# Attention of two heads at a time: scores alternate between the array's row halves, values between its column halves

## The chip, the cores and the metric

One core of one Trainium2 chip runs the whole program. The metric is the device time of one execution in microseconds (us). Three runs of the kernel before took 1670.49, 1671.25 and 1674.58 us, a median of 1671.25 us.

## The reference, cut to what matters

The program is a stack of transformer blocks on 256 tokens of width 1024, all in float32, batch 1. Two layers of the first kind are feed-forward, mixer, feed-forward, each with a residual; two layers of the second kind are one mixer each. The first mixer has three branches, the second has two attentions and a convolution. Heads are 64 wide everywhere, apart from MLA, whose queries and keys are 96 wide:

```
first mixer, a layer:   MLA 6 heads (q, k 96 wide, v 64), MOBA 6 heads,
                        dilated: 4 heads x 3 patterns, joined over the patterns by their log-sum-exp
second mixer, a layer:  FOX 4 heads (bias from cumulated forget gates),
                        NSA 8 heads x 2 sets of keys (selected, window), plus compressed keys
every one of these:     s = q @ k.T * scale + bias;  p = softmax(s, causal);  o = p @ v
```

With 256 tokens MOBA's and NSA's selections hold all blocks, so each attention is a causal one with its own bias. That makes 24 softmax tables of 256x256 per layer in the first mixer (6 + 6 + 12) and 20 in the second (4 + 16), 88 in all.

## The kernel before, in words

**Stages.** The order is feed-forward, first mixer, feed-forward, twice, then the second mixer twice and a last norm (`STAGES`). Every big product is made exactly enough by splitting both operands in two float32r parts and running three matmuls (`mm3`, L229, and `mm3w`, L235; their matmuls are L231 to L233 and L239 to L241). Weights come through one stream (`Stream.emit`, L92): a DMA on SyncE's queue into a `raw` tile of 128x1024, a copy by ScalarE to the high part (`wh`, L110), a subtraction by VectorE to the low part (`wl`, L111). Seven such chunks are kept under way.

**Order.** The Tile framework orders instructions itself: it gives each engine a fixed list, in program order where nothing is waited for by its own timing model, with later instructions put in where an earlier one is not ready. On the chip every engine then runs its list in order. Lower priority is given to the weights' splits (`LOW`). So the projections that stand between attention heads fill the gaps of the heads' chains.

**One head.** `scores` (L534) takes a bank of PSUM from the tag `xt`, of which there are three, and writes the causal half of the table into it: 128 queries against 128 keys (L537) and the other 128 queries against 256 keys (L538). Both are plain float32 matmuls, which the trace records as two passes each. For a head of 64 the operands lie on partitions 0 to 63 or 64 to 127, by the head's parity, so the matmul uses half of the array's rows. `biased` (L543) adds the bias on VectorE and finds the minimum (L546), which frees the bank; `exps` (L552) is ScalarE's Exp (L554); `weighted` (L557) scales the rows on VectorE (L559). `values` (L561) transposes three 128x128 blocks on TensorE into another `xt` bank (L244), copies them to SBUF (ScalarE at L570, for some dilated tables VectorE at L572) into one of two `pt` buffers, and multiplies them with v (L573 and L574), which is 64 columns wide: the output goes to partitions 0 to 63 or 64 to 127 of the one `ot` bank that a pair of heads shares (`pair_out`, L609).

**Lag of one.** `attend` (L576) emits the scores and softmax of a head and then the values of the head before it:

```python
    def attend(self, job):
        first, second = job
        first()
        self.settle()
        self.waiting = second
```

A dilated head does three tables (`dil_job`, L777), with three `p` tiles of six, an NSA head two (`nsa_job`, L1157). After a pair's second head the output bank is split in two parts (L247, L248) or gated (L1154).

**Order around the change.** In the first mixer (L865 to L887) MLA's pairs stand between projections, then MOBA's, then the four gates of branch 0, `dil_pair(0)`, the four gates of branch 1, `dil_pair(1)`, the rest of the values, the four gates of branch 2. A gate (`gated`, L833) is 48 matmuls of gate and some of branch. In the second mixer (L1353 to L1374) FOX and NSA pairs stand between projections, convolution taps on VectorE (`conv`, L1265) and the output product (`outs`).

Of the kernel before, what the change touches and what calls it, by code (L numbers as in the profile page):

```python
# [17 lines left out]
EPS = 1e-6  # L18
# [58 lines left out]
class Stream:  # L77
    """Weights in the order of their use: loaded, and split exactly in two float32r parts."""
# [21 lines left out]
            # a feed-forward's own weights also take turns in the buffers that its pool adds  # L100
# [21 lines left out]
class Next:  # L122
    """what follows a phase, for one block of 128 tokens"""
# [18 lines left out]
class Kernel:  # L142
# [27 lines left out]
    # ------------------------------------------------------------ tiles  # L170
# [32 lines left out]
    def p384(self):  # L203
        return self.lent.tile([128, 384], F32, name="p", bufs=6)
# [23 lines left out]
    # ------------------------------------------------------------ helpers  # L228
# [47 lines left out]
    def setup(self):  # L276
        """what the mixers need"""
# [10 lines left out]
        # rows to columns: the taps, conv_b, ln_g, ln_b of both layers, position embeddings, latent gains  # L288
# [62 lines left out]
    def finish_phase(self, step, n, accs, factor, nxt):  # L351
        """the last n steps of a sum, token block by token block, with the next norm between them"""
# [20 lines left out]
    # ------------------------------------------------------------ feed-forward  # L373
# [21 lines left out]
    def ffn(self, src, pre, nxt, phase, mid):  # L395
# [5 lines left out]
        def finish(j, ga, ua, natural):  # L401
            """silu(gate) * up of 256 columns, transposed and split"""
# [80 lines left out]
    def xs_spec(self, w, c0, n):  # L483
        """the same with the activations stationary"""
# [5 lines left out]
    def ws_proj(self, src, done, i, each=None):  # L490
        """256 columns, transposed: done(i, psum [128, 2, 256])"""
# [12 lines left out]
    def xs_proj(self, src, n, done, pre=None, each=None):  # L504
        """n columns, tokens on partitions: done(t, psum [128, n])"""
# [37 lines left out]
    def biased(self, p, st, table, scale, low):  # L543
        """p = (scores + table) * scale, which is minus the logits; low [128, 2]: their minima"""
# [16 lines left out]
    def values(self, o, p, v, first, last, evac):  # L561
        """o [64, 256] += v.T @ p.T for p [128, 384]"""
        nc = self.nc
        pt = self.xt()
        self.transpose(pt[:, 0:128], p[:, 0:128])
        self.transpose(pt[:, 128:256], p[:, 128:256])
        self.transpose(pt[:, 256:384], p[:, 256:384])
        ps = self.lent.tile([128, 384], F32, name="pt", bufs=2)
        if evac == "a":
            nc.scalar.copy(ps, pt[:, :384])  # L570
        else:
            nc.vector.tensor_copy(ps, pt[:, :384])  # L572
        nc.tensor.matmul(o, lhsT=v[0], rhs=ps[:, 0:256], start=first, stop=False)  # L573
        nc.tensor.matmul(o[:, 128:256], lhsT=v[1], rhs=ps[:, 256:384], start=False, stop=last)  # L574
# [13 lines left out]
    def head(self, q, k, v, o, table, scale, end=None, evac="a"):  # L588
        """o(): psum [64, 256] for the values"""
        p, s = [], []  # L590

        def first():
            st = self.scores(q, k)
            p.append(self.p384())
            s.append(self.small())
            t = table() if callable(table) else table
            self.biased(p[0], st, t, scale, s[0][:, 0:2])
            self.exps(p[0], s[0][:, 0:2], s[0][:, 2:4])
            self.nc.vector.reciprocal(s[0][:, 4:6], s[0][:, 2:4])
            self.weighted(p[0], s[0][:, 4:6])  # L600

        def second():
            self.values(o(), p[0], v, True, True, evac)
            if end:
                end()
# [3 lines left out]
    def pair_out(self):  # L609
        """one psum tile for two heads, made when the first asks for it"""  # L610
# [9 lines left out]
    def rope_pairs(self, a, b, cos, sin, shape):  # L620
        """(a, b) = (a cos - b sin, a sin + b cos) in place"""
# [33 lines left out]
    def mixer1(self, l, src, pre, nxt, mid):  # L655
# [3 lines left out]
        # latent projections, their norms, the shared rotated key  # L659
# [29 lines left out]
        # MOBA queries and keys, transposed, two heads to a block  # L689
# [16 lines left out]
        # MLA heads  # L706
# [48 lines left out]
        def mla_pair(p):  # L755
            o = self.pair_out()
            for m in range(2):
                h = 2 * p + m
                v = [vv[:, t, 64 * h:64 * h + 64] for t in range(2)]
                self.attend(self.head(qT[0:96, h], kT[0:96, h], v, lambda m=m: o(m), self.table(4), 1.0,  # L760
                                      (lambda: finish(0, p, o())) if m else None))

        bv = self.g(9408, 2, 384)

        def moba_pair(p):
            o = self.pair_out()
            for m in range(2):
                h = 2 * p + m
                r = slice(64 * m, 64 * m + 64)
                v = [bv[:, t, 64 * h:64 * h + 64] for t in range(2)]  # L770
                self.attend(self.head(bq[r, p], bk[r, p], v, lambda m=m: o(m), self.table(0), SLOPES[12 + h],
                                      (lambda: finish(1, p, o())) if m else None))
# [4 lines left out]
        def dil_job(p, m, o):  # L777
            j = 2 * p + m
            r = slice(64 * m, 64 * m + 64)
            pp = []  # L780

            def first():
                pp.extend(self.p384() for _ in range(3))
                s = self.small(24)
                low = s[:, 0:6].rearrange("p (g b) -> p g b", b=2)
                den = s[:, 6:12].rearrange("p (g b) -> p g b", b=2)
                for g in range(3):
                    sc = self.scores(dq[r, 2 * g + p], dk[r, 2 * g + p])
                    self.biased(pp[g], sc, self.table(1 + g), SLOPES[4 * g + j], low[:, g])
                lo, dn = s[:, 12:14], s[:, 14:16]  # L790
                nc.vector.tensor_reduce(lo, s[:, 0:6].rearrange("p (g b) -> p b g", b=2), op=OP.min, axis=AX.X)
                for g in range(3):
                    self.exps(pp[g], lo, den[:, g])
                nc.vector.tensor_reduce(dn, s[:, 6:12].rearrange("p (g b) -> p b g", b=2), op=OP.add, axis=AX.X)
                nc.vector.reciprocal(dn, dn)
                for g in range(3):
                    self.weighted(pp[g], dn)

            def second():
                for g in range(3):  # L800
# [672 lines left out]
```

## Time and profile before

| what | value |
|---|---|
| runs, us | 1670.49, 1671.25, 1674.58 |
| span of the profiled execution | 1671.4 us |
| TensorE matmul busy | 1625.8 us, 97% |
| TensorE weight load busy | 1472.4 us, 88% |
| VectorE busy | 1027.7 us, 61% |
| ScalarE busy | 813.5 us, 49% |
| mean DMA rate | 162 GB/s |

The profiled execution's span stands 0.15 us above the median of the runs, so span and time are taken as one. In the trace a matmul has a start and a modelled end; the ends of neighbours overlap, so the cost of one is read from its start to the start of the next, not from its duration. A form such as 64*128 64x256 is the used rows and columns of the array, then partitions and elements of the output's operand.

### The profile page before, as it was taken

What the parts mean: (1) busy time and instruction counts of PE and PEld (TensorE: products, weight loads), DVE (VectorE), ACT (ScalarE), POOL (GpSimd) and SP (SyncE); (2) the same over time, 40 slices, a digit from 0 to 9 for tenths busy, and PEclk for the clock granted to TensorE, in tenths of its full rate; (3) what the DMA queues carried; (4) which work ended last, traced back from release to release, by engine and by line L of the source; (5) the groups of instructions that cost most, each with busy time, mean ns of one, the idle gap of its engine ahead of it and who ended that gap; (6) DMA issues with size and microseconds to landing.
All of it is one profiled execution on the core that took longest, in us unless ns stands there. A gap on an engine that the chain in (4) does not pass through costs nothing.

```text
span 1671.4 us, 28176 instructions
## 1 busy us (share of the span) xinstructions
PE 1625.8 (97%) x11210; PEld 1472.4 (88%) x11210; DVE 1027.7 (61%) x1896; ACT 813.5 (49%) x1365; POOL 70.4 (4%) x76
## 2 busy tenths in 40 slices
PE   6999999999999999999999999999999989999998
PEld 6899999799989999999999799889999788778875
DVE  6655465566675545645456546676544779777885
ACT  5544355554464444444435545555443554555353
POOL 0000000001000000000010000000000011000300
PEclk9999999999999999999999999999999999999999
DMA  8866455344577664766636444477664463246411
GB/s 274 261 187 193 117 168 147 109 140 129 183 214 221 189 186 143 225 186 190 178 97 182 121 136 140 129 222 242 185 190 139 143 201 121 58 122 206 140 43 39
DMA packets 212508, 271.41 MB, mean 162 GB/s; under 512 B 10382, under 2 KB 188440, under 8 KB 212376
## 3 DMA queue, kind: packets, MB, share of 16 engines
q1 hardware_dynamic: 211944, 268.56, 54.0%
q8 instruction: 88, 1.44, 0.4%
q10 hardware_dynamic: 432, 1.05, 0.2%
q14 instruction: 44, 0.36, 0.1%
HBM read 268.52 MB, written 1.05 MB: 161 GB/s over the span
## 4 chain that ended last, share of the span: by engine, by line
PE 83%; DVE 7%; DMA 4%; ACT 2%; issue 2%; POOL 1%; SPq 0%; DVEq 0%; POOLq 0%; ACTq 0%
PE acc L239 16%; PE acc L241 15%; PE acc L240 15%; PE xt L231 4%; PE xt L233 4%; PE xt L232 4%; PE xt L244 3%; PE ot L573 3%; PE acc L231 3%; PE acc L232 3%; PE acc L233 3%; DVE wl L111 2%; PE xt L538 2%; PE xt L537 2%; DMA raw<-in_ffn_w_gate_dram 1%
## 5 line engine op out<-in xcount | busy, mean ns | idle before, releaser
L111 DVE TENSOR_TENSOR wl<-raw,wh 128x1024 fp32r<-128x1024 f32 (+6 forms) x510 | 607.2, 1194 | 449.8 <-ACT wh L110 438.7
L110 ACT CAST wh<-raw 128x1024 fp32r<-128x1024 f32 (+5 forms) x520 | 525.5, 1013 | 589.6 <-PE acc L240 346.7
L239 PE MATMUL acc<-hl,wh 128*128 128x256 f32 x2080 | 594.6, 286 | 0.0
L240 PE MATMUL acc<-hh,wh 128*128 128x256 f32 x2080 | 591.6, 284 | 0.0
L241 PE MATMUL acc<-hh,wl 128*128 128x256 f32 x2080 | 591.2, 284 | 0.0
L239 PEld LDWEIGHTS acc<-hl,wh 128*128 128x128 f32 x2080 | 398.3, 191 | 5.5 <-issue 4.0
L241 PEld LDWEIGHTS acc<-hh,wl 128*128 128x128 f32 x2080 | 398.3, 191 | 4.0 <-issue 4.0
L240 PEld LDWEIGHTS acc<-hh,wh 128*128 128x128 f32 x2080 | 398.3, 191 | 3.2 <-issue 1.7
L231 PE MATMUL acc<-wh,hl 128*128 128x256 f32 (+5 forms) x576 | 189.9, 330 | 2.9 <-DVE hl L248 1.1
L232 PE MATMUL acc<-wh,hh 128*128 128x256 f32 (+5 forms) x576 | 186.2, 324 | 0.0
L233 PE MATMUL acc<-wl,hh 128*128 128x256 f32 (+5 forms) x576 | 185.9, 323 | 0.0
L231 PEld LDWEIGHTS acc<-wh,hl 128*128 128x128 f32 x576 | 109.9, 191 | 13.7 <-issue 3.7
L233 PEld LDWEIGHTS acc<-wl,hh 128*128 128x128 f32 x576 | 109.8, 191 | 6.8 <-issue 1.0
L232 PEld LDWEIGHTS acc<-wh,hh 128*128 128x128 f32 x576 | 110.0, 191 | 6.2 <-issue 1.0
L231 PE MATMUL xt<-wh,R 128*128 128x512 f32 x264 | 103.8, 393 | 1.3 <-DVE R L248 1.3
L232 PE MATMUL xt<-wh,R 128*128 128x512 f32 x264 | 103.5, 392 | 0.0
L233 PE MATMUL xt<-wl,R 128*128 128x512 f32 x264 | 103.3, 391 | 0.0
L554 ACT ACTIVATE p<-p,small 128x128 f32<-128x128 f32 (+1 forms) x176 | 78.6, 448 | 26.8 <-DVE small L546 17.2
L546 DVE CUSTOM_DVE_ANT_0 p<-xt,base 128x128 f32<-128x128 f32 (+1 forms) x160 | 50.9, 352 | 19.0 <-PE xt L538 18.3
L570 ACT COPY pt<-xt 128x384 f32<-128x384 f32 x80 | 37.5, 474 | 49.2 <-PE xt L244 48.0
L231 PEld LDWEIGHTS xt<-wh,R 128*128 128x128 f32 x264 | 49.6, 188 | 11.6 <-DVE R L248 2.3
L233 PEld LDWEIGHTS xt<-wl,R 128*128 128x128 f32 x264 | 49.6, 188 | 10.6
(253 smaller groups left out, 1806.9 us busy)
## 6 DMA issues: line engine op xcount, KB each, us to landing
raw<-in_w_in_dram SPq DMA_DIRECT2D x144, 512.0 KB
raw<-in_ffn_w_gate_dram SPq DMA_DIRECT2D x88, 512.0 KB
raw<-in_ffn_w_up_dram SPq DMA_DIRECT2D x88, 512.0 KB
raw<-in_ffn_w_down_dram SPq DMA_DIRECT2D x88, 512.0 KB
raw<-in_w_out_dram SPq DMA_DIRECT2D x32, 512.0 KB
raw<-in_cmp_k_w_dram SPq DMA_DIRECT2D x8, 512.0 KB
raw<-in_cmp_v_w_dram SPq DMA_DIRECT2D x8, 512.0 KB
raw<-in_w_in_dram SPq DMA_DIRECT2D x8, 416.0 KB
```

The source lines that it names most:

```text
L110: nc.scalar.copy(wh, raw)
L111: (nc.gpsimd if slow else nc.vector).tensor_sub(wl, raw, wh.bitcast(F32))
L231: nc.tensor.matmul(out, lhsT=al, rhs=bh, start=first, stop=False)
L232: nc.tensor.matmul(out, lhsT=ah, rhs=bh, start=False, stop=False)
L233: nc.tensor.matmul(out, lhsT=ah, rhs=bl, start=False, stop=last)
L239: nc.tensor.matmul(out, lhsT=ah, rhs=bl, start=first, stop=False)
L240: nc.tensor.matmul(out, lhsT=ah, rhs=bh, start=False, stop=False)
L241: nc.tensor.matmul(out, lhsT=al, rhs=bh, start=False, stop=last)
L244: self.nc.tensor.transpose(out, in_, self.ident[:rows, :rows])
L546: self.nc.vector.tensor_tensor_reduce(out=p[:, c], in0=st[b], in1=table[b], scale=scale, scalar=3e38, op0=OP.add, op1=OP.min, accum_out=lo ...
L554: self.nc.scalar.activation(p[:, c], p[:, c], AF.Exp, bias=low[:, b:b + 1], scale=-1.0, accum_out=den[:, b:b + 1])
L573: nc.tensor.matmul(o, lhsT=v[0], rhs=ps[:, 0:256], start=first, stop=False)
```

## The change

Heads are handled in pairs. `scores` takes two `xt` banks and issues, in this order, the 128-key matmul of head 0, that of head 1, the 256-key matmul of head 0, that of head 1. `values` transposes and copies both heads' tables, then issues the four products with v in the same alternation. The softmax steps of both heads stand side by side; one reciprocal serves both. `p` gets eight buffers in place of six; `xt` (3), `ot` (1) and `pt` (2) stay. For dilated tables ScalarE copies head 0's transposes and VectorE head 1's. The lag of one is now one pair. `dil_pair(1)` moves from behind the gates of branch 1 into their middle, with the values of pair 0 right before it. Comments are dropped throughout.

```diff
     def p384(self):
-        return self.lent.tile([128, 384], F32, name="p", bufs=6)
+        return self.lent.tile([128, 384], F32, name="p", bufs=8)
-    def scores(self, q, k):
-        nc, st = self.nc, self.xt()
-        nc.tensor.matmul(st[:, 0:128], lhsT=q[:, 0:128], rhs=k[:, 0:128], start=True, stop=True)
-        nc.tensor.matmul(st[:, 128:384], lhsT=q[:, 128:256], rhs=k[:, 0:256], start=True, stop=True)
-        return [st[:, c] for c in self.PARTS]
+    def scores(self, qs, ks):
+        nc, st = self.nc, [self.xt(), self.xt()]
+        for c, at, n in ((self.PARTS[0], 0, 128), (self.PARTS[1], 128, 256)):
+            for m in range(2):
+                nc.tensor.matmul(st[m][:, c], lhsT=qs[m][:, at:at + 128], rhs=ks[m][:, 0:n], start=True, stop=True)
+        return [[st[m][:, c] for c in self.PARTS] for m in range(2)]
-    def values(self, o, p, v, first, last, evac):
...
+    def values(self, o, ps, vs, first, last, evac):
+        nc, pts = self.nc, []
+        for m in range(2):
+            pt = self.xt()
+            for i in range(3):
+                c = slice(128 * i, 128 * i + 128)
+                self.transpose(pt[:, c], ps[m][:, c])
+            pts.append(self.lent.tile([128, 384], F32, name="pt", bufs=2))
+            (nc.scalar.copy if evac[m] == "a" else nc.vector.tensor_copy)(pts[m], pt[:, :384])
+        for m in range(2):
+            nc.tensor.matmul(o(m), lhsT=vs[m][0], rhs=pts[m][:, 0:256], start=first, stop=False)
+        for m in range(2):
+            nc.tensor.matmul(o(m)[:, 128:256], lhsT=vs[m][1], rhs=pts[m][:, 256:384], start=False, stop=last)
+    def heads(self, qs, ks, vs, tables, scales, end):
...
+            st = self.scores(qs, ks)
+            ps.extend(self.p384() for _ in range(2))
+            for m in range(2):
+                t = tables[m]() if callable(tables[m]) else tables[m]
+                self.biased(ps[m], st[m], t, scales[m], w[:, 2 * m:2 * m + 2])
+            for m in range(2):
+                self.exps(ps[m], w[:, 2 * m:2 * m + 2], w[:, 4 + 2 * m:6 + 2 * m])
+            self.nc.vector.reciprocal(w[:, 8:12], w[:, 4:8])
+            for m in range(2):
+                self.weighted(ps[m], w[:, 8 + 2 * m:10 + 2 * m])
...
         for c in range(4):
+            if c == 2:
+                self.settle()
+                dil_pair(1)
             gated(1, c)
-        dil_pair(1)
         self.settle()
```

`dil_pair` and `nsa_pair` are rewritten in the same manner: for each pattern or set of keys the scores of both heads, then the softmax of both; for the values, one call of `values` per pattern or set of keys.

## Rows read from the trace of the kernel before

**Rows 1.** The page: busy time and share of the span, by engine.

```profile
PE 1625.8 (97%) x11210; PEld 1472.4 (88%) x11210; DVE 1027.7 (61%) x1896; ACT 813.5 (49%) x1365; POOL 70.4 (4%) x76
```

**Rows 2.** Windows: length, busy us (count) PE, PEld, DVE, ACT, POOL; clock, DMA, GB/s.

```profile
212.00:461.00 249.00, 248.42 (x1779) 225.99 (x1777) 149.74 (x317) 127.84 (x258) 8.58 (x10) 1.00 0.51 147
...
1391.00:1471.00 80.00, 77.55 (x455) 58.33 (x454) 64.96 (x221) 44.58 (x126) 7.45 (x6) 1.00 0.24 71
...
1575.00:1654.00 79.00, 78.58 (x460) 59.01 (x460) 60.87 (x221) 41.86 (x123) 8.86 (x6) 1.00 0.12 39
```

**Rows 3.** Waits of TensorE: total us, times, longest us.

```profile
PE ot L573 <- ACT pt L570: 1.6, 2, 1.3
```

**Rows 4.** Groups by line and form, TensorE: busy us, mean ns of one pass.

```profile
L573 PE MATMUL ot<-pt,G 128*64 128x256 f32 x176 | 56.3, 401 | 2.2 <-ACT pt L570 1.6
...
L538 PE MATMUL xt<-G 64*128 64x256 f32 x152 | 44.9, 378 | 0.0
...
L537 PE MATMUL xt<-G 64*128 64x128 f32 x152 | 34.3, 307 | 0.0
```

**Rows 5.** Timeline of TensorE, dilated scores: start us, us, line, form, passes.

```profile
363.16 0.38 PE L537 MATMUL xt<-G 64*128 64x128 f32 x2
...
363.81 0.38 PE L537 MATMUL xt<-G 64*128 64x128 f32 x2
364.03 0.38 PE L538 MATMUL xt<-G 64*128 64x256 f32 x1
364.06 0.37 PE L537 MATMUL xt<-G 64*128 64x128 f32 x1
364.25 0.38 PE L538 MATMUL xt<-G 64*128 64x256 f32 x1
364.27 0.27 PE L537 MATMUL xt<-G 64*128 64x128 f32 x1
364.38 0.59 PE L538 MATMUL xt<-G 64*128 64x256 f32 x2
```

**Rows 6.** Timeline of TensorE around one head's scores (FOX).

```profile
1393.26 0.28 PE L240 MATMUL acc<-hh,wh 128*128 128x256 f32 x1
1393.47 0.49 PE L537 MATMUL xt<-G 64*128 64x128 f32 x2
1393.79 0.59 PE L538 MATMUL xt<-G 64*128 64x256 f32 x2
1394.32 0.39 PE L241 MATMUL acc<-hh,wl 128*128 128x256 f32 x1
1394.54 0.28 PE L239 MATMUL acc<-hl,wh 128*128 128x256 f32 x1
```

**Rows 7.** Timeline of TensorE around one head's values (MLA).

```profile
272.45 0.28 PE L240 MATMUL acc<-hh,wh 128*128 128x256 f32 x1
272.57 0.28 PE L241 MATMUL acc<-hh,wl 128*128 128x256 f32 x1
272.78 0.65 PE L573 MATMUL ot<-pt,G 128*64 128x256 f32 x2
273.26 0.38 PE L574 MATMUL ot<-pt,G 128*64 128x128 f32 x2
273.57 0.39 PE L239 MATMUL acc<-hl,wh 128*128 128x256 f32 x1
273.79 0.28 PE L240 MATMUL acc<-hh,wh 128*128 128x256 f32 x1
```

**Rows 8.** Timeline of VectorE while dilated scores are drained.

```profile
363.92 1.22 DVE L111 TENSOR_TENSOR wl<-raw,wh 128x1024 fp32r<-128x1024 f32 x1
365.05 0.28 DVE L546 CUSTOM_DVE_ANT_0 p<-xt,base 128x128 f32<-128x128 f32 x1
...
365.61 0.29 DVE L546 CUSTOM_DVE_ANT_0 p<-xt,base 128x128 f32<-128x128 f32 x1
```

**Rows 9.** Groups by line: ScalarE's copy of the transposes, VectorE's reciprocal.

```profile
L570 ACT COPY pt<-xt 128x384 f32<-128x384 f32 x80 | 37.5, 474 | 49.2 <-PE xt L244 48.0 <-PE ot L574 1.0
...
L599 DVE RECIPROCAL small<-small 128x2 f32<-128x2 f32 x32 | 5.2, 162 | 7.4 <-ACT p L554 6.9
```

More of the change, by code (lines that the diff above doesn't have):

```diff
@@ L586, in settle @@
         self.waiting = None
-    def head(self, q, k, v, o, table, scale, end=None, evac="a"):
-        p, s = [], []
+    def heads(self, qs, ks, vs, tables, scales, end):
+        ps, s = [], []
         def first():
[L593 to L600, printed above, removed]
+            st = self.scores(qs, ks)
+            ps.extend(self.p384() for _ in range(2))
+            w = self.small(12)
+            s.append(w)
+            for m in range(2):
[6 more added lines that the diff above has]
+                self.weighted(ps[m], w[:, 8 + 2 * m:10 + 2 * m])
         def second():
-            self.values(o(), p[0], v, True, True, evac)
-            if end:
-                end()
+            o = self.pair_out()
+            self.values(o, ps, vs, True, True, "aa")
+            end(o())
         return first, second
@@ L755, in mla_pair @@
         def mla_pair(p):
[L756 to L761, printed above, removed]
+            hs = (2 * p, 2 * p + 1)
+            self.attend(self.heads([qT[0:96, h] for h in hs], [kT[0:96, h] for h in hs],
+                                   [[vv[:, t, 64 * h:64 * h + 64] for t in range(2)] for h in hs],
+                                   [self.table(4)] * 2, (1.0, 1.0), lambda o: finish(0, p, o)))
@@ L763, in mixer1 @@
         bv = self.g(9408, 2, 384)
+        HALVES = (slice(0, 64), slice(64, 128))
         def moba_pair(p):
[L766 to L772, printed above, removed]
+            hs = (2 * p, 2 * p + 1)
+            self.attend(self.heads([bq[r, p] for r in HALVES], [bk[r, p] for r in HALVES],
+                                   [[bv[:, t, 64 * h:64 * h + 64] for t in range(2)] for h in hs],
+                                   [self.table(0)] * 2, [SLOPES[12 + h] for h in hs], lambda o: finish(1, p, o)))
@@ L774, in mixer1, with dil_pair @@
         dv = self.g(6144, 2, 768)
         dq, dk = self.g(0, 6, 256), self.g(1536, 6, 256)
-        def dil_job(p, m, o):
-            j = 2 * p + m
-            r = slice(64 * m, 64 * m + 64)
+        def dil_pair(p):
             pp = []
             def first():
[L783 to L786, printed above, removed]
+                s = self.small(32)
+                low = s[:, 0:12].rearrange("p (m g b) -> p m g b", m=2, b=2)
+                den = s[:, 12:24].rearrange("p (m g b) -> p m g b", m=2, b=2)
+                lo, dn = (s[:, i:i + 4].rearrange("p (m b) -> p m b", m=2) for i in (24, 28))
@@ L795, in first @@
[L795 to L800, printed above, removed]
-                    h = 4 * g + j
-                    self.values(o(m), pp[g], [dv[:, t, 64 * h:64 * h + 64] for t in range(2)], g == 0, g == 2,
-                                "ad"[g % 2])
-                if m:
-                    finish(2, p, o())
-            return first, second
-        def dil_pair(p):
-            o = self.pair_out()
-            for m in range(2):
-                self.attend(dil_job(p, m, o))
+                    pp.append([self.p384() for _ in range(2)])
@@ new lines, in first @@
+                    sc = self.scores([dq[r, 2 * g + p] for r in HALVES], [dk[r, 2 * g + p] for r in HALVES])
+                    for m in range(2):
+                        self.biased(pp[g][m], sc[m], self.table(1 + g), SLOPES[4 * g + 2 * p + m], low[:, m, g])
+                for m in range(2):
+                    nc.vector.tensor_reduce(lo[:, m], low[:, m].rearrange("p g b -> p b g"), op=OP.min, axis=AX.X)
+                    for g in range(3):
+                        self.exps(pp[g][m], lo[:, m], den[:, m, g])
+                    nc.vector.tensor_reduce(dn[:, m], den[:, m].rearrange("p g b -> p b g"), op=OP.add, axis=AX.X)
+                    nc.vector.reciprocal(dn[:, m], dn[:, m])
+                    for g in range(3):
+                        self.weighted(pp[g][m], dn[:, m])
@@ L814, in moba_v, with second @@
+            def second():
+                o = self.pair_out()
+                for g in range(3):
+                    hs = (4 * g + 2 * p, 4 * g + 2 * p + 1)
+                    self.values(o, pp[g], [[dv[:, t, 64 * h:64 * h + 64] for t in range(2)] for h in hs], g == 0,
+                                g == 2, "ad")
+                finish(2, p, o())
+            self.attend((first, second))
         def moba_v(t, a):
@@ L1165, in first @@
                 for i in range(2):
-                    sc = self.scores(qT[r, p], kT[r, g, i])
-                    self.biased(pp[i], sc, self.table(4), 1.0, s[:, 2 * i:2 * i + 2])
+                    sc = self.scores([qT[r, p] for r in HALVES], [kT[r, g, i] for r in HALVES])
+                    for m in range(2):
+                        self.biased(pp[i][m], sc[m], self.table(4), 1.0, low[:, m, i])
                 for i in range(2):
-                    self.exps(pp[i], s[:, 2 * i:2 * i + 2], s[:, 4 + 2 * i:6 + 2 * i])
@@ L1173, in first @@
                 for i in range(2):
-                    self.weighted(pp[i], w[:, i])
+                    for m in range(2):
+                        self.weighted(pp[i][m], w[:, m, i])
             def second():
-                if m == 0:
-                    nc.tensor.matmul(o(), lhsT=vbd[:, 2 * p:2 * p + 2].rearrange("p a b -> p (a b)"), rhs=pcT,
-                                     start=True, stop=False)
+                o = self.pair_out()
+                nc.tensor.matmul(o(), lhsT=vbd[:, 2 * p:2 * p + 2].rearrange("p a b -> p (a b)"), rhs=pcT,
+                                 start=True, stop=False)
@@ L1180, in second @@
                 for i in range(2):
                     c = (384, 640)[i] + 64 * g
-                    self.values(o(m), pp[i], [nk[:, t, c:c + 64] for t in range(2)], False, i == 1, "a")
-                if m:
-                    gated_out(4 + p, o(), sn[:, p])
-            return first, second
-        def nsa_pair(p):
-            o = self.pair_out()
-            for m in range(2):
-                self.attend(nsa_job(p, m, o))
+                    self.values(o, pp[i], [[nk[:, t, c:c + 64] for t in range(2)]] * 2, False, i == 1, "aa")
@@ L1194, in fox_qk @@
+                gated_out(4 + p, o(), sn[:, p])
+            self.attend((first, second))
         def fox_qk(i, a):
@@ new lines, in fox_pair, with table @@
+            hs = (2 * p, 2 * p + 1)
+            def table(h):
+                ck = self.xt()[:, :256]
+                nc.tensor.matmul(ck, lhsT=ls[:, 0, h:h + 1].to_broadcast([128, 128]), rhs=self.tri, start=True,
+                                 stop=False)
+                nc.tensor.matmul(ck[:, 128:256], lhsT=ls[:, 1, h:h + 1].to_broadcast([128, 128]),
+                                 rhs=self.tri[:, 0:128], start=False, stop=True)
+                bt = self.gt(512)
+                t0, t1 = self.table(4)
+                nc.vector.scalar_tensor_tensor(bt[:, 0:128], ck[:, 0:128], cq[:, 0, h:h + 1], t0,
+                                               op0=OP.subtract, op1=OP.add)
+                nc.vector.scalar_tensor_tensor(bt[:, 128:384], ck, cq[:, 1, h:h + 1], t1, op0=OP.subtract,
+                                               op1=OP.add)
+                return [bt[:, c] for c in self.PARTS]
@@ L1252, in silu_gate @@
+            self.attend(self.heads([fq[r, p] for r in HALVES], [fk[r, p] for r in HALVES],
+                                   [[fv[:, t, 64 * h:64 * h + 64] for t in range(2)] for h in hs],
+                                   [lambda h=h: table(h) for h in hs], (1.0, 1.0),
+                                   lambda o: gated_out(p, o, sf[:, p])))
         def silu_gate(dst):
```

59 lines of the change are left out of this document (13 added, 46 removed).

## The prediction

> **What bounds the kernel now.** I read the page first: TensorE is busy for 97% of the span, every other engine for 61% or less [rows 1]. The list of TensorE's waits then shows that the attention hardly stops it: all waits for a copied table of weights are two, 1.6 us in sum [rows 3]. The windows of the stretches with attention, third, show where TensorE alone is the bound. In the first mixer of a layer it is busy for 248.42 of 249 us, with VectorE at 149.74 and ScalarE at 127.84 us; the reader is to see that a microsecond taken off TensorE is gained there, since the others have a third and more of the time to spare. In the second mixer's attention it is busy for 77.55 of 80 and 78.58 of 79 us, but VectorE has 64.96 and 60.87 us of work in them [rows 2], so there not much can be taken off before VectorE is next. Last comes the timeline of TensorE, for what attention costs in its queue.
>
> **What a head costs TensorE.** A head's 128 and 256 columns, in two passes each, take 0.65 us from start to start (363.16 to 363.81) [rows 5]. Of the scores, 152 passes of each kind have 64 rows [rows 4], which is 76 heads' tables or 38 pairs; the rest are MLA's 96-row ones, which don't fit in half of the rows. The values are 176 passes of each kind [rows 4], 44 pairs. The same columns in the same passes take the values 0.65 us too. On top comes the change of the array's form. One head's scores between projections take from 1393.26 to 1394.54, 1.28 us, of which 0.65 is its own and two times 0.12 the projections' (a projection matmul takes 0.12, as from 272.45 to 272.57 [rows 7]): 0.39 us for going in and out [rows 6]. A head's values take from 272.57 to 273.79, 1.22 us, so 0.33 us for in and out [rows 7]. In TensorE's timeline I count 58 such stretches of scores and 73 of values.
>
> **Do halves run side by side?** For rows the trace has one place where the last matmul of one head stands before the first of the other: 364.03 and 364.06, then the second passes at 364.25 and 364.27 [rows 5]. The two heads' passes start 0.02 to 0.03 us apart, where a second pass in the same half waits 0.22 us. So alternating scores of two heads take the time of one. For columns no two heads' values stand next to each other in this trace; the gain is bounded by nothing and by 0.65 us a pair.
>
> **The change part by part.**
> - Scores, 0.65 us saved per pair that really alternates. The two banks that a pair needs are free for its first table: MOBA 6 pairs, dilated 4, FOX 4, NSA 8, so 22 x 0.65 = 14.3 us. The 16 later tables (dilated 8, NSA 8) find one bank of three free; the second head's waits until VectorE has drained one, and the list is then likely to have this head's matmuls in a row. I take a quarter, 16 x 0.65 / 4 = 2.6 us; ends 0 and 10.4. MLA's 6 pairs: nothing.
> - Values. ScalarE copies head 0's table and then head 1's, 0.47 us each [rows 9]; the order of instructions is greedy, so head 0's first product goes out when its copy is there and its second one follows before head 1's copy has landed. What can then overlap is the second product of head 0 with the first of head 1, 0.22 us, and only where nothing came between. I take that for half of the 44 pairs: 4.8 us. Ends: 0 and 44 x 0.65 = 28.6 us; I stay near the lower one as no row shows an overlap of columns.
> - Fewer changes of form. At best one stretch per pair: 38 and 44. Since banks and copies will split some, I take 45 and 55: 13 x 0.39 + 18 x 0.33 = 11.0 us. Ends 0 and 20 x 0.39 + 29 x 0.33 = 17.4.
> - Softmax on VectorE and ScalarE: the same counts, but 16 of 32 reciprocals of 0.16 us go [rows 9], and four dilated copies move from ScalarE to VectorE. Neither engine is the path in the first mixer, so 0; if that cover goes, 2.6 us less on VectorE against some 2 us more.
> - `dil_pair(1)` between the gates of branch 1: it issues no DMA, so SyncE's queue keeps its order, and nothing on GpSimd. Its 12 tables' scores, biases, exponentials and scalings now stand ahead of two gates' tanh and products, which are covered by 96 projection matmuls of 0.12 us (11.5 us). 0.
> - A new wait. A pair's values want two `xt` banks while the next pair's scores hold two; the second head's transposes wait for a drained bank, and they also fill both `pt` buffers, so the next table's copies wait for this one's products. VectorE drains a head in 0.56 us (365.05 to 365.61) [rows 8]. Behind the waiting transposes in TensorE's list stand projections, and ScalarE's copy waits for them. In the first mixer the list puts projections in front, so 0; in the second there are few left. I take one drain for each of the 8 NSA pairs, 4.5 us; ends 0 and one for all 44, 24.6 us.
>
> **Sum.** On TensorE 14.3 + 2.6 + 4.8 + 11.0 = 32.7 us. The second mixer's share is 12 of the 22 first tables (7.8), 8 of 16 later ones (1.3), 20 of 44 values (2.2) and about half of the changes of form (5.5): 16.8, or 8.4 a layer. Taking 8.4 off 80 us would leave VectorE busy for 65 of 71.6 us, with chains in it that can't be packed so; I count half, and lose 8.4. What is late next there is VectorE. 32.7 - 8.4 - 4.5 = 19.8 us off the profiled 1671.4 us: 1651.6. The median of the runs is 0.15 us lower: **1651.5 us**, 1.2% faster.
>
> **Rivals.**
> - Values one after the other. The column halves might not overlap at all, as each product needs all rows. Then 4.8 us on TensorE are lost, of which 2.2 in the second mixer count half: 19.8 - 3.7 gives 1655. For it: the timeline shows side by side only what differs in rows. Against: nothing either. A rule of the Trainium skill (TensorE: Matmul & The Clock Gate, Part 3, "The mechanism") says this: a weight load runs beside matmuls in flight only where its group of rows is another one. No run here shows it for columns; by the same part's table of packings, columns gain nearly what rows do.
> - Everything overlaps. All ends of the gains: 14.3 + 10.4 + 28.6 + 17.4 = 70.7 us, half of the second mixer's 34 lost: 1618 us. For it: rows 5, and TensorE's 97%. Against: three banks and the one copy at a time.
> - It doesn't do what it says: the order splits each pair's matmuls by head, in scores as well, and each split costs a change of form as before. 1671 us, within 5 us. For it: the one place of rows 5 is the only such meeting among 76 tables. Against: both banks are free at most pairs' starts.
> - Slower. TensorE stands at the second head's transposes while VectorE, which owes the bank, is at a weight subtraction of 1.22 us (363.92) before its drain [rows 8]: 1.78 us. In the first mixer projections cover it; in the second, where VectorE has 65 of 80 us, 20 pairs x 1.78 = 35.6 us stand against gains of 24.3: 1682 us. It decides from 14 of the 20 pairs on. Against: the 1.6 us of rows 3.
>
> **How the numbers follow.** A measurement of this kernel tells 0.3%, 5 us, from no change. Forecast 0.40, values one after the other 0.18, everything overlaps 0.17, doesn't do what it says 0.12, slower 0.13. The first three are faster by more than 5 us: 0.75; within 0.12; slower 0.13. The range reaches down to 1618, the sum of all ends, leaving out half of that case, and up to 1676, leaving out the slower case: 1618 to 1676 holds 0.8.
>
> **What would show it.** Right: first tables of MOBA, FOX and NSA pairs show both heads' 64-row matmuls 0.02 us apart; some 45 stretches of scores and 55 of values; in the values an overlap of head 0's second with head 1's first product; the first mixers shorter by 8 us each, the second mixers by 4. Wrong in the large: alternating values that start together (then it goes to 1618), or TensorE waiting for VectorE at L546 or for ScalarE at the copies by more than 10 us in sum (then towards 1682), or scores in head order.

## The result and the profile after

The changed kernel takes **1648.3 us** (median of 4 executions, 1646.28 to 1650.84) against 1671.35 us before (4 executions): ratio 0.9859, 95% interval 0.9845 to 0.9874. It is faster by 23 us, where 19.8 were predicted. An execution's time lies 1.8 us above its span; the profiled one took 1649.59 us with a span of 1647.8 us.

The page's busy times, against [rows 1]:

```profile
PE 1595.3 (97%) x11210; PEld 1451.0 (88%) x11210; DVE 1024.6 (62%) x1876; ACT 809.7 (49%) x1361; POOL 73.8 (4%) x76
```

TensorE issues the same 11210 passes in 30.5 us less. Its groups by line and form, against [rows 4] (L573, L538 and L537 there):

```profile
L573 PE MATMUL ot<-pt,G 128*64 128x256 f32 x176 | 46.4, 406 | 2.7 <-ACT pt L571 2.3
...
L539 PE MATMUL xt<-G 64*128 64x256 f32 x152 | 33.4, 382 | 0.0
...
L539 PE MATMUL xt<-G 64*128 64x128 f32 x152 | 27.0, 317 | 0.3
```

Counts are as before and means of one pass nearly so (401, 378 and 307 ns there), and the busy times are 10 us, 11.5 us and 7 us lower. Busy time counts a moment once, however many passes are under way in it. So a lower busy time at the same count and mean says that passes of a group overlap more: in the scores, as forecast, and as much in the values, which was not. It doesn't say that they run side by side, since the modelled ends of mere neighbours overlap too. The kernel with the same columns (below), in which no two products with v start together, still stands under the 56.3 us of before:

```profile
L573 PE MATMUL ot<-pt,G 128*64 128x256 f32 x176 | 52.5, 401 | 3.0 <-ACT pt L571 2.5
```

What runs side by side is read from starts, as follows.

The windows that answer to [rows 2] (length, busy us and count of PE, PEld, DVE, ACT, POOL, then granted clock, DMA share, GB/s):

```profile
212.00:461.00 249.00, 247.59 (x1813) 225.77 (x1814) 152.07 (x323) 131.08 (x264) 10.95 (x11) 1.00 0.51 149
1379.00:1459.00 80.00, 73.78 (x474) 56.41 (x473) 68.02 (x218) 44.72 (x127) 8.91 (x10) 0.98 0.26 76
1556.00:1633.00 77.00, 73.25 (x477) 55.76 (x476) 64.00 (x218) 42.36 (x125) 9.40 (x6) 1.00 0.16 50
```

The first mixer is still TensorE's alone. In the second mixers TensorE now stands for 6.2 of 80 and 3.8 of 77 us. Its list of waits says for what:

```profile
PE xt L1233 <- DVE gt L1241: 5.4, 3, 2.0
...
PE ot L573 <- ACT pt L571: 2.3, 4, 0.9
```

The second line is [rows 3] over again. The first stood at 0.9 us, once, before: TensorE wants an `xt` bank for the bias table of FOX's second head (L1233), and the bank is freed by VectorE's work on the first head's table (L1241).

### Where TensorE's time went

In the timeline of TensorE I added up the stretches of 64-row scores and of products with v, from the first pass of a stretch to the end of its last (its start and its own length), and apart from that what going in and out of a stretch costs beyond the neighbours' own length. A pass "meets" its neighbour if they start within 0.06 us.

| | scores: stretches, us inside, meetings, in and out | values: the same |
|---|---|---|
| before | 54, 54.8, 4, 10.1 | 73, 61.7, 0, 17.5 |
| changed | 42, 40.6, 86, 8.2 | 63, 45.7, 67, 16.2 |

That is 16.1 us saved in the scores and 17.3 in the values, 33.4 in sum. By stage (a stage ends with VectorE's last addition to `x` but one), in the profiled executions:

| us | first mixers | second mixers | span |
|---|---|---|---|
| before | 261.7, 261.9 | 183.8, 179.4 | 1671.4 |
| changed | 254.8, 254.8 | 181.0, 172.5 | 1647.8 |
| same rows | 257.2, 257.3 | 178.2, 172.8 | 1649.9 |
| same columns | 257.6, 257.7 | 184.8, 178.2 | 1661.9 |
| same rows and columns | 259.6, 259.7 | 185.8, 178.6 | 1666.9 |
| bias tables first | 254.7, 254.8 | 176.6, 170.5 | 1640.3 |
| all three edits | 252.4, 251.2 | 176.1, 172.2 | 1634.6 |

The feed-forwards agree within 1.3 us in all of them.

### The profile page after: what moved, and what is told of

It is laid out like the page before. It is cut to its first block, busy times and chain, and to the rows that moved or that the text cites. A ratio compares the mean times of both kernels' runs of the same rounds, so it can differ in the third digit from the quotient of the medians.

```text
span 1647.8 us, 28135 instructions
## 1 busy us (share of the span) xinstructions
PE 1595.3 (97%) x11210; PEld 1451.0 (88%) x11210; DVE 1024.6 (62%) x1876; ACT 809.7 (49%) x1361; POOL 73.8 (4%) x76
## 4 chain that ended last, share of the span: by engine, by line
PE 80%; DVE 10%; DMA 4%; ACT 3%; issue 2%; POOL 1%; SPq 0%; DVEq 0%; POOLq 0%; ACTq 0%
PE acc L239 15%; PE acc L240 15%; PE acc L241 15%; PE xt L231 4%; PE xt L233 4%; PE xt L232 4%; PE xt L244 3%; PE acc L231 3%; DVE wl L111 3%; PE acc L233 3%; PE xt L539 3%; PE acc L232 3%; PE ot L573 2%; ACT wh L110 1%; DMA raw<-in_ffn_w_gate_dram 1%
## 5 line engine op out<-in xcount | busy, mean ns | idle before, releaser
L231 PEld LDWEIGHTS xt<-wh,R 128*128 128x128 f32 x264 | 49.6, 188 | 11.1 <-DVE R L248 1.8
L233 PEld LDWEIGHTS xt<-wl,R 128*128 128x128 f32 x264 | 49.6, 188 | 10.6
L232 PEld LDWEIGHTS xt<-wh,R 128*128 128x128 f32 x264 | 49.6, 188 | 9.2
L539 PE MATMUL xt<-G 64*128 64x256 f32 (+3 forms) x352 | 56.0, 346 | 0.3
```

Of the source, the lines that this page charges most:

```text
L231: nc.tensor.matmul(out, lhsT=al, rhs=bh, start=first, stop=False)
L232: nc.tensor.matmul(out, lhsT=ah, rhs=bh, start=False, stop=False)
L233: nc.tensor.matmul(out, lhsT=ah, rhs=bl, start=False, stop=last)
L539: nc.tensor.matmul(st[m][:, c], lhsT=qs[m][:, at:at + 128], rhs=ks[m][:, 0:n], start=True, stop=True)
```

## The experiments

**Theory:** both halves of the array, rows and columns, take two heads' passes side by side, and that is nearly all of the gain. **Rivals:** columns don't run side by side, and the saving in the values is order (fewer, longer stretches); or the moved dilated pair, or copies that are further ahead.

### Rows and columns, each taken away, and both

Same rows (both heads' scores from the first head's rows; the order of instructions stays as in the changed kernel):

```diff
-                nc.tensor.matmul(st[m][:, c], lhsT=qs[m][:, at:at + 128], rhs=ks[m][:, 0:n], start=True, stop=True)
+                nc.tensor.matmul(st[m][:, c], lhsT=qs[0][:, at:at + 128], rhs=ks[0][:, 0:n], start=True, stop=True)
```

> The scores of both heads of a pair are computed from the operands of head 0, so both lie in the same half of the rows; everything else, the order of the instructions on every engine too, is that of the kernel after, and the second heads' results are left out of the sum of what is computed. Theory (rows side by side carry a part of the gain): no two 64-row matmuls start within 0.06 us of each other (86 do after), the stretches of scores take 13 us more of TensorE, and the time is 7 to 13 us above that of after, 1655 to 1661 us. Rival (the gain is fewer changes of form and a better order): within 3 us of after, 1645 to 1651 us.

1652.8 us, ratio to before 0.9886 (0.9871 to 0.99). The meetings went and the 13 us came, as expected; the time stayed 2 us under the expected range (why, below). Same columns (both heads' values into one column half; VectorE clears the other where there is one table; the order shifts in places, with 66 stretches of values in place of 63):

```diff
-            nc.tensor.matmul(o(m), lhsT=vs[m][0], rhs=pts[m][:, 0:256], start=first, stop=False)
+            nc.tensor.matmul(o(half), lhsT=vs[m][0], rhs=pts[m][:, 0:256], start=first and m == 0, stop=False)
...
-            nc.tensor.matmul(o(m)[:, 128:256], lhsT=vs[m][1], rhs=pts[m][:, 256:384], start=False, stop=last)
+            nc.tensor.matmul(o(half)[:, 128:256], lhsT=vs[m][1], rhs=pts[m][:, 256:384], start=False, stop=last and m == 1)
```

> Both heads' products with v are written to one and the same column half (the lower for a pair with one table and for every other table); the placement of the second head's values in its own half is left out, and VectorE clears the unused half where there is only one table. The number of products, their sizes and the copies they wait for stay. Theory (the 14 us that TensorE saves in the products with v are two column halves running side by side): no product with v starts within 0.06 us of its neighbour's start any more (67 in the changed kernel), the time inside the stretches of products with v goes from 45.7 us to about 60, each first mixer gets 3 to 4 us longer (254.8 to about 258.5), each second mixer 0 to 4, and the whole 1655 to 1663. Rival (the saving comes from fewer and longer stretches, and the column halves have no part in it): stretches about 46 us as before, first mixers within 1 us of 254.8, the whole at most 1651.

1663.51 us, ratio 0.9962 (0.9947 to 0.9976), half a microsecond above what was expected. And both edits in one kernel, in the order of the one just shown:

> The run above with, beside it, both heads' scores taken from the first head's rows, as in the first run of this study (the second head's scores are left out as such): the instructions and their order are those of the run above, and nothing can run side by side in either array half. Theory (nearly all the gain is side by side running): first mixers about 261 us each (254.8 after, 261.7 before), the whole 1660 to 1670, so that only the 3 to 8 us of fewer changes of form are left of the gain. Rival (half or more of the gain is order alone: fewer changes of form and copies that are further ahead): at most 1657, first mixers at most 259.

1669.28 us (10 executions), ratio 0.9996 (0.9986 to 1.0006): no different from the kernel before.

TensorE's timeline (start, length, line, form, passes) of one pair's values, in the changed kernel:

```profile
379.39 0.28 PE L241 MATMUL acc<-hh,wl 128*128 128x256 f32 x1
379.73 0.65 PE L573 MATMUL ot<-pt,G 128*64 128x256 f32 x4
380.21 0.39 PE L575 MATMUL ot<-pt,G 128*64 128x128 f32 x4
380.54 0.66 PE L244 MATMUL xt<-ident,p 128*128 128x128 f32 x4
```

and in the kernel with the same columns:

```profile
380.68 0.28 PE L241 MATMUL acc<-hh,wl 128*128 128x256 f32 x1
381.02 1.08 PE L573 MATMUL ot<-pt,G 128*64 128x256 f32 x4
381.94 0.60 PE L575 MATMUL ot<-pt,G 128*64 128x128 f32 x4
382.47 0.33 PE L244 MATMUL xt<-ident,p 128*128 128x128 f32 x1
```

The four long passes take 0.48 us (379.73 to 380.21) in two column halves and 0.92 us (381.02 to 381.94) in one; 0.48 us is what one head's two took before (272.78 to 273.26) [rows 7]. Their weight loads (PEld) do the same, in the changed kernel and in the one with the same columns:

```profile
379.73 0.20 PEld L573 LDWEIGHTS ot<-pt,G 128*64 128x64 f32 x4 [0.26 <-ACT pt L571]
```

```profile
381.02 0.62 PEld L573 LDWEIGHTS ot<-pt,G 128*64 128x64 f32 x4 [0.26 <-ACT pt L571]
```

A modelled length says little here: read from start to start. A pair's scores do the same in rows. The changed kernel, then the one with the same rows:

```profile
312.53 0.39 PE L233 MATMUL acc<-wl,hh 128*128 128x512 f32 x1
312.85 0.93 PE L539 MATMUL xt<-G 64*128 64x128 f32 x8
313.70 0.55 PE L244 MATMUL xt<-ident,p 128*128 128x128 f32 x3
```

```profile
313.22 0.39 PE L233 MATMUL acc<-wl,hh 128*128 128x512 f32 x1
313.54 1.57 PE L539 MATMUL xt<-G 64*128 64x128 f32 x8
315.04 0.33 PE L244 MATMUL xt<-ident,p 128*128 128x128 f32 x1
```

0.85 us against 1.50 us, 0.65 less, as the prediction had it. Over the program, the scores with the same rows take 54.1 us inside their stretches with no meeting (40.6 and 86 in the changed kernel), the values with the same columns 60.8 with none (45.7 and 67). So of the 33.4 us, 13.5 are rows side by side, 15.1 columns, and 4.8 remain for everything else. The rival of order alone falls.

In the program's time rows look smaller than that: 4.5 us from 1648.3 to 1652.8. Other things moved in that run too, all of them in its favour. Its values, which the edit doesn't touch, meet 87 times in place of 67 and cost 2.1 us less with in and out, and the wait at L1233 fell from 5.4 to 4.0 us. And TensorE's clock interferes (see the last section). An execution's mean granted clock is 0.992 to 0.996 in the changed kernel's four, and 0.994 to 0.997 with the same rows; a thousandth of it over the span is 1.65 us. Brought to 0.994 by that (an estimate), the medians are: before 1672, same rows and columns 1671.9, same columns 1662.7, same rows 1655.9, changed 1647.7. Each half can be taken away with the other there or gone: rows give 8 to 9 us (1671.9 to 1662.7, 1655.9 to 1647.7), columns 15 to 16 (1671.9 to 1655.9, 1662.7 to 1647.7). In the first mixers, where the clock stood at 1.00, no correction is needed: the same rows cost 2.4 and 2.5 us a mixer, the same columns 2.8 and 2.9, and with both 2.1 us are left of the 7.

### Order of the values

```diff
-        for m in range(2):
-            nc.tensor.matmul(o(m)[:, 128:256], lhsT=vs[m][1], rhs=pts[m][:, 256:384], start=False, stop=last)
+            nc.tensor.matmul(o(m)[:, 128:256], lhsT=vs[m][1], rhs=pts[m][:, 256:384], start=False, stop=last)
```

(both products of a head, then both of the other)

> The four products with v of a pair are issued head by head in place of alternating. Theory (columns side by side carry a part of the gain): at most one overlap a pair is left, TensorE spends 5 to 13 us more in the values, 1653 to 1661 us. Rival (column halves gave nothing, the values are set by the copies): within 3 us of after, or faster, as head 0's products no longer wait for head 1's copy.

1644.89 us, ratio 0.9834 (0.9817 to 0.985): if anything faster, each first mixer by 1.0 us. The expectation failed. In the changed kernel the commonest split is this one (MLA):

```profile
281.53 0.65 PE L573 MATMUL ot<-pt,G 128*64 128x256 f32 x2
282.10 0.39 PE L239 MATMUL acc<-hl,wh 128*128 128x256 f32 x1
282.33 0.28 PE L240 MATMUL acc<-hh,wh 128*128 128x256 f32 x1
282.54 0.43 PE L573 MATMUL ot<-pt,G 128*64 128x256 f32 x1
282.55 0.43 PE L575 MATMUL ot<-pt,G 128*64 128x128 f32 x2
282.81 0.38 PE L573 MATMUL ot<-pt,G 128*64 128x256 f32 x1
283.02 0.38 PE L575 MATMUL ot<-pt,G 128*64 128x128 f32 x2
```

Head 0's long product goes alone, projections fill the time until head 1's copy has landed, and then head 1's product meets head 0's short one (282.54 and 282.55). Of the 44 pairs I count 19 split so, and 7 in which all passes meet. By head, the values need 46 stretches in place of 63: meetings fall to 57 and the time inside rises to 49.1 us, but in and out falls from 16.2 to 12.6, so the values cost the same with in and out (61.7 and 61.9). What TensorE does save lies in the scores (46.9 against 48.8 us with in and out), which the values no longer split so often. Two further tries on the copies:

```diff
-            self.values(o, ps, vs, True, True, "aa")
+            self.values(o, ps, vs, True, True, "ad")
```

(NSA likewise: VectorE copies the second head's table)

> Head 1's transposes are copied by VectorE everywhere, not for dilated tables alone. Theory (head 1's copy, one ScalarE copy behind head 0's, keeps most pairs from overlapping fully): the starts within 0.06 us in the values go from 67 to over 120, values stretches from 63 to about 50, and the time is 5 to 12 us shorter, 1636 to 1643 us. Rival (in the second mixer VectorE is next): 28 copies of 0.56 us on VectorE cost there what they give, 1646 us or more.

1656.7 us, ratio 0.9908 (0.9893 to 0.9923), slower than the changed kernel: the rival came out, and the theory (more meetings) not, with 66 of them. The values fell into 78 stretches, with 50.6 us inside, and the second mixers took 185.0 and 175.3 us. That the copies queue behind VectorE's other work is likely, but no line of the waits shows it. And a head's products right behind its copy, ahead of the next head's transposes:

```diff
-        for m in range(2):
             nc.tensor.matmul(o(m), lhsT=vs[m][0], rhs=pts[m][:, 0:256], start=first, stop=False)
-        for m in range(2):
             nc.tensor.matmul(o(m)[:, 128:256], lhsT=vs[m][1], rhs=pts[m][:, 256:384], start=False, stop=last)
```

(both now in the loop of the transposes)

> Head 0's transposes, copy and two products stand before head 1's, so that the products of a pair meet only by chance; scores stay paired. Theory (columns side by side are worth about 15 us of TensorE, and the by-head run kept one meeting a pair): starts within 0.06 us in the values fall from 67 to under 20, the values take over 8 us more than after, and the first mixers are longer by 3 us or more each: 1654 to 1660 us. Rival (the order of transposes and copies matters more than any overlap): as with products by head, 1645 us or less.

1647.84 us, ratio 0.9866 (0.9852 to 0.9879). It decided nothing: the framework moved the products together again, and 54 meetings stayed, where under 20 were expected.

### The moved dilated pair

```diff
-            if c == 2:
-                self.settle()
-                dil_pair(1)
             gated(1, c)
+        self.settle()
+        dil_pair(1)
```

> The second dilated pair goes back behind all four gates of branch 1, with the first pair's values right before it. Theory (the move was covered by projections and costs or gives nothing): within 2 us of after, 1646 to 1650 us. Rival (the move feeds TensorE with attention while gates are left to fill its gaps, and is a part of the gain): the first mixers grow by 1.5 us or more each, 1651 us or more.

1646.47 us, ratio 0.986 (0.9846 to 0.9873): the same as the changed kernel. The move is worth nothing, as predicted.

### The new wait at FOX

```diff
+            made = [t() if callable(t) else t for t in tables]
             st = self.scores(qs, ks)
...
-                t = tables[m]() if callable(tables[m]) else tables[m]
+                t = made[m]
```

> In FOX both heads' bias tables are made before the pair takes its two score banks. Theory (second head's table waits for the third bank, behind VectorE, 5.4 us in three waits): that wait falls under 1.5 us, 1643 to 1645 us. Rival (the wait only moves, to the scores that then wait for a bank, or to VectorE): within 2 us of after, 1646 to 1650 us.

1641.87 us, ratio 0.9821 (0.9806 to 0.9836). The theory held, and the time lies 1 us under its range: L1233's wait is gone, and 1.1 us stand in its place:

```profile
PE xt L539 <- DVE gt L1242: 1.1, 1, 1.1
```

In the changed kernel the longest of the three looks like this, TensorE and then VectorE:

```profile
1392.50 0.28 PE L241 MATMUL acc<-hh,wl 128*128 128x256 f32 x1
1394.81 0.67 PE L1233 MATMUL xt<-tri,G 128*128 128x256 f32 x2 [2.03 <-DVE gt L1241]
```

```profile
1390.41 3.01 DVE L1270 SCALAR_TENSOR_TENSOR G<-G,conv 128x256 f32<-128x256 f32 x2
1393.34 0.68 DVE L1255 SCALAR_TENSOR_TENSOR G<-gt,acc 128x512 f32<-128x512 f32 x1
1393.94 0.34 DVE L1239 SCALAR_TENSOR_TENSOR gt<-xt,G,base 128x128 f32<-128x128 f32 x1
1394.20 0.47 DVE L1241 SCALAR_TENSOR_TENSOR gt<-xt,G,base 128x256 f32<-128x256 f32 x1
```

Two heads' scores and the first bias table hold all three `xt` banks. The work that frees one (L1239, L1241) stands behind two convolution taps that take 3.01 us. With the clock brought to 0.994 as above, the run is 4.4 us below the changed kernel, about as much as these waits fell (5.4 to 1.1 us), although its scores meet 72 times, not 86, and take 2.3 us more. The second mixers now lie 7.2 and 8.9 us below the kernel before (of the 8.9, 1.7 are one fall of the clock less). TensorE's own saving in them, added up as in the first table, is some 7.4 and 8.5 us in this run, and 9.7 and 10.0 in the changed kernel.

### Dilated scores, and what adds up

The 24 passes of a dilated pair hardly gained. The changed kernel, from 358.83 to 362.45:

```profile
358.83 3.69 PE L539 MATMUL xt<-G 64*128 64x128 f32 x24
362.45 0.39 PE L239 MATMUL acc<-hl,wh 128*128 128x256 f32 x1
```

With the second head's scores in a bank of the other ring, in the first mixers:

```diff
-        nc, st = self.nc, [self.xt(), self.xt()]
+        nc, st = self.nc, [self.xt(), self.acc(512) if self.phase == "m" else self.xt()]
```

> In the first mixer the second head's scores take a bank of the projections' four in place of a third of the three. Theory (three banks keep the dilated tables after the first from alternating): the starts within 0.06 us in the scores go up by 20 or more, the first mixers are 1.5 to 3 us shorter each, 1642 to 1645 us. Rival (the projections need their four banks, or VectorE sets the pace of these tables): first mixers within 1 us of after or longer, 1647 us or more.

1640.75 us, ratio 0.9823 (0.981 to 0.9836), and the same 24 passes from 356.11 to 358.27:

```profile
356.11 0.37 PE L539 MATMUL xt<-G 64*128 64x128 f32 x1
356.12 0.37 PE L539 MATMUL acc<-G 64*128 64x128 f32 x1
...
358.27 0.39 PE L239 MATMUL acc<-hl,wh 128*128 128x256 f32 x1
```

2.16 us against 3.62: with one bank more every pass of this pair meets its partner. The meetings in the scores rose from 86 to 102, a little less than expected, and the time fell a little more. The first mixers took 251.7 and 254.1 us; in the second of them the clock fell once.

Values by head and bias tables first, together:

> Products with v by head and FOX's bias tables before the scores, together. Theory (the two act in different stages, the one in the first mixers, the other in the second): the gains add, 3.4 + 6.4 us off after, 1637 to 1640 us. Rival (both only shake the order of the second mixer): no better than tables first alone, 1641 us or more.

1640.97 us, ratio 0.9821 (0.9807 to 0.9834), within the noise of the tables alone. With the other ring's bank besides:

> Three edits that were each faster alone: values one head after the other, both bias tables asked for ahead of the first head's multiplication, and the second head's scores in a bank of the other ring in the first mixers. Theory (they take away different waits, so the gains add): first mixers 251 to 252 us, second mixers 176 and 170 to 172, the whole 1634 to 1637. Rival (they take away the same slack, as two of them did when joined): 1640 or more, first mixers 253 or more.

**1635.64 us** (1634.56 to 1636.49), ratio 0.9794 (0.978 to 0.9809), the best version here, 35 us below the kernel before and, by the two intervals, below the changed one. Each alone against the changed kernel, the three gave 3.4, 6.4 and 7.6 us, 17.4 in sum; together they give 12.7. So most of it adds up, not all; what values by head gives beyond the tables is not resolved.

Last, in the first mixers, products over all 128 columns, half of whose result is thrown away:

```diff
+        if wide:
+            for m in range(2):
+                oc = o()[:, 256 * m:256 * m + 256]
+                nc.tensor.matmul(oc, lhsT=wide[0], rhs=pts[m][:, 0:256], start=first and m == 0, stop=False)
+                nc.tensor.matmul(oc[:, 128:256], lhsT=wide[1], rhs=pts[m][:, 256:384], start=False,
+                                 stop=last and m == 1)
+            return
```

> In the first mixers alone each head's product with v uses all 128 columns of the array (the values of both heads side by side as weights), and each head's half of the result is taken from its own part of a bank twice as wide; the other half of the result is thrown away. Nothing runs side by side there and the array keeps its form; each pair's result is split by twice as many operations, half as many partitions each. Theory (in the changed kernel the meeting products and their changes of form together cost about as much as four full-width passes each): 24 pairs at 0.65 us are 15.6 us against 17.1 us a mixer after, so each first mixer 0 to 2 us shorter, second mixers as after, the whole 1644 to 1649. Rival (column halves running side by side are worth more than the form, or the doubled split operations are late): first mixers 2 us longer or more, the whole 1651 or more.

1646.27 us, ratio 0.9859 (0.9844 to 0.9873), first mixers 255.0 and 255.0: a tie. Keeping the array's form is worth there about what running side by side is with one meeting in most pairs (35 of 44 in the changed kernel).

## Why the prediction was right, and where not

The time (1651.5 against 1648.3, inside 1618 to 1676) and the sign are right, and so is the mechanism: the halves do run side by side. The sum is nearer than its terms, and that is luck: on TensorE 32.7 us were forecast and 33.4 saved, with the values 10.3 us too low and the scores and the changes of form together 9.6 too high.

- **Scores, 16.9 us.** 13.5 us on TensorE and 8 to 9 in the time, too much. The first tables were right: 0.65 us for a pair. The later ones gave little; the six meetings in the dilated 24 passes are what a third bank allows.
- **Values, 4.8 us.** The mis-sized term: 15.1 us on TensorE, 15 to 16 in the time, the largest part of the gain. I stayed near the lower end because no row showed columns side by side. That head 0's second product meets head 1's first was right, but not the half of pairs: 35 of the 44 have one meeting, and 7 have all four. The rival "values one after the other" falls. The rule of the Trainium skill that I named for it (TensorE: Matmul & The Clock Gate, Part 3, "The mechanism") does not hold for the column halves here, where four weight loads lay within 0.20 us in place of 0.62 and their passes took 0.48 us in place of 0.92. The same part's table of packings, by which columns gain nearly what rows do, does.
- **Fewer changes of form, 11.0 us.** 4.8 us at most on TensorE. There are 42 stretches of scores (45 expected) and 63 of values (55); four of the 58 that I counted before were another product's. And in and out of a stretch costs less than 0.39 and 0.33 us: with what the first pass loses it is 0.28 and 0.30 by the table (10.1 and 5.2 us, the 54.8 less the passes' own 49.6, over 54 stretches; 17.5 and 4.3 over 73).
- **Second mixers, half lost (8.4), and the new wait (4.5).** The size was about right: 33.4 us saved, 23.6 off the span, so 9.8 lost against 12.9. The cause was another. VectorE's load doesn't take back what TensorE saves: once the FOX tables are asked for first, 7.2 us arrive in each (clock set apart), nearly all that TensorE saves there in that run, with VectorE's load as before. Copies moved to VectorE did cost time, though: 8.4 us, from 1648.3 to 1656.7. And the wait is not at NSA's transposes but at FOX's bias table, which I did not count as a user of the third `xt` bank; it is a wait for VectorE, by the order of its list. First mixers gained 7 each (8 forecast), second 2.8 and 6.9 (4 each).
- **Softmax and the moved pair, 0.** The move is shown to be nothing by its own run. The softmax was not tried apart; VectorE's and ScalarE's sums moved by 3 and 4 us.

## What to carry to other kernels

Products that use half of the array's rows or half of its columns can run two at a time, if the two halves' passes stand next to each other in TensorE's list and their operands are there together; so count the PSUM banks and copies that a pair needs at once, and every other user of that ring. Test such an overlap by giving both the same half: counts stay, the order nearly so, and the side by side running goes. Look, too, at what else such a test moves: here the other half's meetings and a wait. Judge a few microseconds in stages where the granted clock stands at 1.00, or note the clock beside the time.

## What the runs showed of the hardware

**Column halves run side by side** in two-pass float32 products (0.48 us for four passes, 0.92 in one half), though each of these products uses all 128 rows.

**The clock fell behind one wait and not behind its like.** In the second mixers the granted clock drops at times from 2.4 GHz to its lower level, 1.2 GHz; a window whose granted clock lies between 0.5 and 1 holds some of both. Windows of the changed kernel, the first of them the wait shown above:

```profile
1392.60:1394.80 2.20, 0.18 (x2) 0.02 (x1) 2.20 (x7) 0.00 (x0) 0.53 (x1) 1.00 0.73 205
1394.80:1397.00 2.20, 2.19 (x11) 2.15 (x12) 1.88 (x10) 1.41 (x6) 0.00 (x0) 0.63 0.51 205
1397.00:1399.00 2.00, 2.00 (x8) 1.13 (x7) 1.42 (x5) 1.16 (x5) 0.00 (x0) 0.55 0.00 0
1399.00:1401.00 2.00, 2.00 (x15) 1.52 (x15) 0.58 (x3) 0.26 (x2) 0.00 (x0) 1.00 0.00 0
```

After the 2.03 us of standing, 0.63 and 0.55 over 4.2 us cost 1.7 us of full-speed work (0.37 x 2.2 + 0.45 x 2.0): wait and fall together cost nearly twice the wait's length. But the kernel with the same columns has the same wait of 2.03 us, ending at 1398.77, and no fall behind it:

```profile
1399.00:1401.00 2.00, 2.00 (x15) 1.63 (x14) 1.87 (x10) 1.65 (x7) 0.00 (x0) 1.00 0.45 182
1401.00:1403.00 2.00, 2.00 (x12) 1.28 (x12) 2.00 (x7) 1.12 (x5) 0.00 (x0) 1.00 0.00 0
```

Added up in 2 us windows, the clock took 6.8 us from the first of the second mixers in the changed kernel, 3.4 before, 3.4 with the bias tables first and 1.7 with the same rows. So 5.1 us of clock hid what the same rows cost there. What decides whether a wait is followed by a fall stays open.
